# Layer 2's gates by tokens, an earlier x tile, a last gate item between two pooling items, and a margin for TensorE's choice of line

## Chip, core and metric

The kernel runs on one core of one Trainium2 chip. The metric is the device time of one execution in microseconds. The kernel before has a median of 1224.74 us in 3 runs (1224.27 to 1226.64). Its profiled execution took 1224.48 us; the profiled span is 1222.7 us, so 1.78 us lie around the span.

## The reference

Two layers work on 1040 tokens (16 meta tokens and 1024 of the sequence) of width 1024. Each has 4 heads of forgetting attention ("fox"), 4 heads of differential attention and a pooling mixer; they are gated, joined and projected back.

```python
for l in range(DEPTH):                                   # 2 layers
    hn = rmsnorm(h, norm_g[l])
    proj = einsum('bld,de->ble', hn, w_in[l])
    fq, fk, fv, fz, fg, dq, dk, dv, dz, pu, pz = split(proj)
    log_f = log_sigmoid(fg + b_f[l])                     # 4 gates per token
    c = transpose(cumsum(log_f, axis=1))                 # added to the fox scores
    a_out = forgetting_attention(fq, fk, fv, c) * silu(fz)
    b_out = rmsnorm(differential_attention(dq, dk, dv, lam), subln_g[l]) * (1 - lambda_init) * silu(dz)
    c_out = pooling_mixer(pu, w_pool[l], pool_scale[l]) * silu(pz)
    h = h + einsum('ble,ed->bld', concatenate([a_out, b_out, c_out]), w_out[l])
y = rmsnorm(h[:, N_META:N_META + S], final_g)
```

The pooling mixer takes means over windows of 2, 4, 8 and 16 tokens, subtracts the input, multiplies by a 64x64 matrix per group and scales each channel with `pool_scale`.

## The kernel before

**Tiles.** Activations are kept transposed in `HT`, with 1024 channels in 8 blocks of 128 partitions and 1040 tokens along the free axis. Values are split into a high and a low part, and each product is made of three (high by high, high by low, low by high). ACT copies the high part out of PSUM, DVE subtracts it from PSUM to give the low part; for weights ACT makes the high part and POOL the low one (`ws<-wr,ws`). Projections run over the tokens in three chunks of 346 to 348 columns, in blocks of 128 output channels. PSUM tiles are named by use: `psP` projections, `psS` scores and transposes into `HT`, `psT` transposes of probabilities (`p`) and of gates, `psO` attention outputs.

**Stages of a layer.** First come the norm and the transposes into `HT` (in layer 2 these run beside the output projection of layer 1, tile by tile), and the four gates per token. Then six attention units follow, two of fox and four of differential attention; while a unit's attention runs, the projections of the next unit are the filler. Beside unit 5 the filler is a list of items: the z gate of the unit, two pooling items (`pool_item` 1 and 0, each of two groups) and two z gates of the pooling. Last is the output projection.

**The gates.** Layer 1 projects them (`psP<-HT,wg`, 36 columns of weights, three chunks of tokens). Layer 2 sums products on DVE into `gt`, 128 tokens by 9 tiles by 4 gates (`next_gates`, line 743). Its `end()` transposes the nine 128x4 pieces on PE, ACT adds the bias on the way to the row tile `gx` of 4x1040, and `gate_sums` (line 773) makes `mn`, `na`, two passes of ACT (Exp and Ln), a subtraction and a scan along the 1040 tokens. The result `mn` is stored to `c_d` in DRAM by SP and read back as `cb`, spread over 128 partitions, which the fox softmax of DVE adds to the scores (`p<-psS,cb`).

**Meta keys.** `meta_t` (line 1000) transposes the probabilities of the 16 meta tokens into `psT` and makes the tile `ptm` of 96 partitions, which is a high part, a low part and the high part again (lines 1009 to 1011).

**What sets the order.** The program is first written out by a planner. Class `Order` (line 160) then collects every instruction with an estimated duration and plays a list schedule. `prepare` computes from each instruction the longest way to the end. `simulate` takes on each engine the instruction that can start first, the one with the longest way where several can. On PE there are up to six lines, each in its own order, and the choice is only which line goes next. `tell` then fixes this order on the chip. All engines and SP's DMA queue so run in a fixed order, and an instruction that waits holds back what stands behind it on its engine. Matmuls are at line 517 of the profile, transposes on PE at line 523, everything else at line 151.

Of the kernel before, what the change touches and what calls it, by code (L numbers as in the profile page):

```python
# [161 lines left out]
class Order:  # L162
# [5 lines left out]

    def __init__(self):
        self.ops, self.writes, self.reads, self.rings, self.place = [], {}, {}, {}, {}  # L170
        self.stream = 0
# [32 lines left out]
    def add(self, eng, ins, outs, inps, dur, port=False):  # L204
        k, before, names = len(self.ops), set(), set()
        for aps, own, others in ((inps, self.reads, (self.writes,)), (outs, self.writes, (self.writes, self.reads))):
            for ap in aps:
                name = ap.tensor.name
                names.add(name)
                p0, p1, at = self.parts(ap)  # L210
                if self.place.get(name, ("",))[0] == "VM":
                    p0, p1, at = 0, 128, [(0, 1 << 20)]
                for lo, hi in at:
                    for other in others:
                        old = other.get(name, ())
                        before.update(e[4] for e in old if e[2] < hi and lo < e[3] and e[0] < p1 and p0 < e[1])
                        if own is self.writes and old:
                            other[name] = [e for e in old if e[0] < p0 or e[1] > p1 or e[2] < lo or e[3] > hi]
                    own.setdefault(name, []).append((p0, p1, lo, hi, k))
# [16 lines left out]
    def cost(eng, op, out, ins, extra, kw):  # L236
# [16 lines left out]
        if not sbuf or op == "tensor_tensor_scan":  # L253
            return 150 + 1.05 * n, False
# [6 lines left out]
    def prepare(self):  # L261
# [12 lines left out]
        for o in ops:  # L274
            for b in o["before"]:
                ops[b]["after"].append(o["k"])

        last = None
        for o in reversed(ops):
            way = max((ops[a]["way"] for a in o["after"]), default=0.0)  # L280
            for n in o["tiles"]:
                tag, i = self.place[n]
                bufs, names = self.rings[tag]
                if i + bufs < len(names) and self.first[names[i + bufs]] > o["k"]:
                    way = max(way, ops[self.first[names[i + bufs]]]["way"])
            way += o["end"]
            if o["eng"] == "pe":
                if last is not None:
                    way = max(way, last + o["dur"])
                last = way  # L290
            o["way"] = way

    def simulate(self):
        ops = self.ops
        self.prepare()
# [45 lines left out]
        while n_done < len(ops):  # L341
            best = None
            for e in engines:
                if e == "pe":
                    c = None
                    for line in lines.values():
# [3 lines left out]
                        d = (t, 0.0, line[-1], t, e)  # L350
                        if c is None or d < c:
                            c = d
                    if c is None:
                        continue
                else:
# [71 lines left out]
def hymba(  # L427
# [315 lines left out]
    def next_gates(l):  # L743

        bf = small.tile([4, 1], F32, tag="bf", name=nm("bf"), bufs=2)
        sync.dma_start(bf, b_f[l].rearrange("(f o) -> f o", o=1))
        gx = row("gx")[:4]
# [4 lines left out]
        gt = small.tile([128, 9, 4], F32, tag="gt", name=nm("gt"), bufs=1)  # L752
        done = []
# [9 lines left out]
        def end():  # L763
            with ordr.line(4):
                for g, np_, col in done:
                    pt = psT()[:4, :np_]
                    transpose(pt, g, identf[:np_, :np_])
                    act.activation(gx[:, col : col + np_], pt, AF.Identity, bias=bf)
            gate_sums(l, gx)
# [161 lines left out]
    def task_steps(st, jp, m, idx):  # L931
# [70 lines left out]
        def meta_t():  # L1002
# [6 lines left out]
            act.activation(ptm[0:32], pt, AF.Copy)  # L1009
            dve.tensor_tensor(out=ptm[32:64], in0=pt, in1=f32(ptm[0:32]), op=ALU.subtract)  # L1010
            act.activation(ptm[64:96], pt, AF.Copy)
# [454 lines left out]
    HT = big.tile([128, 2, 8, T], F32R, name="HT")  # L1466
    g = load_g(norm_g[0])
# [26 lines left out]
    for l in range(DEPTH):  # L1494
# [29 lines left out]
        for u in range(6):  # L1524
# [6 lines left out]
            else:  # L1531
                Y = []
                more += [pool_item(l, t, Y) for t in (1, 0)] + [pool_gate(l, t, Y) for t in (1, 0)]
# [15 lines left out]
    ordr.simulate()  # L1549
# [42 lines left out]
```

## Time and profile before

| | us |
|---|---|
| median of 3 runs | 1224.74 |
| profiled execution | 1224.48 |
| its span | 1222.7 |
| PE busy | 1188.7 |
| DVE busy | 814.0 |
| ACT busy | 658.3 |
| POOL busy | 493.5 |

An engine is busy while the profile shows an instruction on it. A line of the timeline gives the start, the time until the end of the group, the engine, the source line, the operation, what is written and read, the shape, the count, and in brackets the idle time before it with the instruction that ended it. The waits view sums these idle times. The windows view cuts the span into stretches and gives each engine's busy time in them.

### The profile page before, as it was taken

Reading aid. Unit: us, or ns where it says so; the run is one execution under the profiler, and the core shown is the slowest. Engines: PE = TensorE matmul, PEld = TensorE weight load, DVE = VectorE, ACT = ScalarE, POOL = GpSimd, SP = SyncE. Lnnn points to the kernel's source line nnn. Section 1 sums busy time; section 2 is a strip of 40 time slices with the busy share of each in tenths; the row PEclk is TensorE's granted clock in tenths of the full one; section 3 lists DMA queues with packets and bytes.
Section 4 is the critical chain, followed back from the end, with each engine's and each line's share of the span. In section 5 each row is a group of like instructions: output and inputs, shape, how many; then the busy total and the mean of one; then the engine's idle time right before and its main releaser. Section 6 shows DMA issues by size and latency. Waiting matters only on the chain.

```text
span 1222.7 us, 21035 instructions
## 1 busy us (share of the span) xinstructions
PE 1188.7 (97%) x7605; PEld 1120.7 (92%) x7605; DVE 814.0 (67%) x2137; ACT 658.3 (54%) x1536; POOL 493.5 (40%) x572
## 2 busy tenths in 40 slices
PE   5999999999999999899999999999999999999997
PEld 4999999999999999878889899999999999998886
DVE  6557567675766767667886675676768585777422
ACT  6556556565555654552235565665655555556322
POOL 4331623336162542465425234252443526235532
PEclk9999999999999999999999999999999999999999
DMA  7120211121222263472110212111223223325431
GB/s 244 27 71 18 59 47 27 45 44 32 53 40 61 35 126 78 136 237 80 67 53 18 71 36 69 27 27 53 30 42 61 40 50 65 78 50 158 140 108 52
DMA packets 101273, 84.21 MB, mean 69 GB/s; under 512 B 18296, under 2 KB 90232, under 8 KB 101168
## 3 DMA queue, kind: packets, MB, share of 16 engines
q1 hardware_dynamic: 101024, 82.60, 26.5%
q8 instruction: 60, 0.98, 0.3%
q14 instruction: 45, 0.37, 0.1%
q10 hardware_dynamic: 144, 0.26, 0.1%
HBM read 69.00 MB, written 13.80 MB: 68 GB/s over the span
## 4 chain that ended last, share of the span: by engine, by line
PE 86%; DVE 5%; ACT 3%; DMA 2%; issue 2%; SPq 1%; POOL 1%; POOLq 0%; ACTq 0%; DVEq 0%
PE psP L517 55%; PE psS L517 15%; PE psO L517 8%; PE psT L523 7%; DVE p L151 1%; SPq L151 1%; DMA r_d<-rs 1%; PE psS L523 1%; PE psT L517 1%; ACT K L151 1%; DVE K L151 1%; DMA sc<-in_pool_scale_dram 1%; ACT ptm L151 0%; DMA x<-in_x_dram 0%; DVE ptm L151 0%
## 5 line engine op out<-in xcount | busy, mean ns | idle before, releaser
L517 PE MATMUL psP<-HT,ws 128*128 128x346 f32 (+5 forms) x4032 | 730.3, 325 | 3.9 <-DVE K L151 2.0
L517 PEld LDWEIGHTS psP<-HT,ws 128*128 128x128 f32 x4032 | 636.5, 188 | 6.5 <-issue 2.3
L151 POOL TENSOR_TENSOR ws<-wr,ws 128x512 fp32r<-128x512 f32 x112 | 150.0, 1342 | 263.3 <-ACT ws L151 203.0
L151 POOL TENSOR_TENSOR q<-rq,q 64x256 fp32r<-64x256 f32 (+1 forms) x192 | 147.9, 770 | 124.7 <-DVE q L151 104.2
L151 ACT ACTIVATE p<-p,mx 128x144 f32<-128x144 f32 (+3 forms) x192 | 150.5, 784 | 49.3 <-DVE mx L151 48.3
L517 PE MATMUL psS<-K,q 128*128 128x392 f32 (+9 forms) x696 | 146.7, 324 | 1.0 <-DVE mx L151 0.8
L151 DVE TENSOR_TENSOR pp<-psT,pp 128x512 fp32r<-128x512 f32 (+1 forms) x160 | 99.2, 634 | 46.7 <-ACT pp L151 45.0
L517 PE MATMUL psO<-pp,VV 128*128 128x256 f32 (+1 forms) x800 | 129.2, 283 | 0.2
L523 PE MATMUL psT<-identf,p 128*128 128x128 f32 (+1 forms) x704 | 114.5, 273 | 3.3 <-DVE p L151 3.0
L151 ACT ACTIVATE pp<-psT 128x512 fp32r<-128x512 f32 (+1 forms) x160 | 85.4, 551 | 60.0 <-PE psT L523 55.9
L517 PE MATMUL psP<-HT,ms 128*128 128x512 f32 (+1 forms) x504 | 115.0, 385 | 0.5 <-POOL ms L151 0.3
L517 PEld LDWEIGHTS psO<-pp,VV 128*128 128x128 f32 x800 | 113.1, 189 | 2.0 <-DVE pp L151 0.9
L517 PEld LDWEIGHTS psS<-K,q 128*128 128x128 f32 (+1 forms) x696 | 108.4, 186 | 4.7 <-DVE mx L151 2.7
L517 PEld LDWEIGHTS psP<-HT,ms 128*128 128x128 f32 x504 | 90.7, 188 | 20.7 <-POOL ms L151 0.8
L523 PEld LDWEIGHTS psT<-identf,p 128*128 128x128 f32 (+1 forms) x704 | 81.3, 132 | 10.8 <-DVE p L151 4.7
L151 ACT ACTIVATE ws<-wr 128x512 fp32r<-128x512 f32 x112 | 70.0, 628 | 33.4 <-PE psP L517 18.4
L151 ACT ACTIVATE ptm<-psT 32x256 fp32r<-32x256 f32 (+1 forms) x128 | 47.5, 371 | 63.1 <-DVE ptm L151 45.0
L517 PE MATMUL psS<-HT,ms 128*128 128x512 f32 (+2 forms) x320 | 75.4, 394 | 0.0
L151 DVE TENSOR_SCALAR p<-p,rd 128x144 f32<-128x144 f32 (+7 forms) x128 | 72.3, 568 | 1.7
L517 PEld LDWEIGHTS psS<-HT,ms 128*128 128x128 f32 (+2 forms) x320 | 57.5, 180 | 16.7
L151 DVE TENSOR_TENSOR K<-psP,K 64x346 fp32r<-64x346 f32 (+1 forms) x72 | 37.2, 517 | 47.4 <-ACT K L151 46.8
L151 POOL TENSOR_TENSOR ms<-mr,ms 128x128 fp32r<-128x128 f32 (+2 forms) x39 | 39.1, 1010 | 68.7 <-ACT ms L151 68.6
(138 smaller groups left out, 1423.0 us busy)
## 6 DMA issues: line engine op xcount, KB each, us to landing
wr<-in_w_in_dram SPq DMA_DIRECT2D x112, 256.0 KB, 2.8
wo<-in_w_out_dram SPq DMA_DIRECT2D x14, 512.0 KB, 5.3
mr<-mix_d SPq DMA_DIRECT2D x14, 320.0 KB, 4.5
cb<-c_d SPq DMA_DIRECT2D x8, 520.0 KB
x<-in_x_dram SPq DMA_DIRECT2D x8, 512.0 KB, 6.5
res<-in_x_dram SPq DMA_DIRECT2D x8, 512.0 KB
h_d<-res SPq DMA_DIRECT2D x8, 512.0 KB, 2.6
res<-h_d SPq DMA_DIRECT2D x8, 512.0 KB, 4.6
```

The lines of the kernel that those rows point to most:

```text
L151: r = f(*args, **kw)
L517: r = nc.tensor.matmul(o, w, m, start=start, stop=stop)
L523: r = nc.tensor.transpose(o, src, ident)
```

## The change

1. PE's choice between its lines compares the times at which their heads are ready plus 400 ns (`SPARE`); an instruction that has been ready for less than 400 ns when PE gets free counts as later. The planned start is still the real one.
2. `ptm` counts as one tile in the order's dependencies, and in `meta_t` the second ACT copy stands before DVE's subtraction.
3. The scan has a cost of its own in the order's estimates.
4. `prepare` is split. `weigh` computes the ways, from the second round on in the order of the starts just planned; `choose` runs up to 6 rounds of `weigh` and `simulate` and keeps the round that ends first by the estimates.
5. In layer 2 the bias, the minimum, Exp, Ln and the subtraction of the gates work on `gt` (128x36) before the nine transposes. Behind the transposes only ACT's copies, the scan and the store remain.
6. The x tile 0 is loaded ahead of `g`.
7. Beside unit 5 the items are pool item 1, z gate of the unit, pool item 0, and the two pooling gates; before, the z gate came first.

```diff
+    SPARE = 400
...
-                if self.place.get(name, ("",))[0] == "VM":
+                if self.place.get(name, ("",))[0] in ("VM", "ptm"):
...
-        if not sbuf or op == "tensor_tensor_scan":
+        if op == "tensor_tensor_scan":
+            return 150 + 2.1 * n, True
+        if not sbuf:
             return 150 + 1.05 * n, False
...
+    def weigh(self):
+        ops, last = self.ops, None
+        for o in reversed(ops if self.start is None else sorted(ops, key=lambda o: (self.start[o["k"]], o["k"]))):
+            after = o["after"] + [self.first[self.heir[n]] for n in o["tiles"] if n in self.heir]
+            way = max((ops[a].get("way", 0.0) for a in after), default=0.0) + o["end"]
             if o["eng"] == "pe":
                 if last is not None:
                     way = max(way, last + o["dur"])
                 last = way
             o["way"] = way
+    def choose(self, rounds):
+        self.prepare()
+        best = None
+        for _ in range(rounds):
+            self.weigh()
+            end = self.simulate()
+            if best is None or end < best[0]:
+                best = end, self.start, self.done, self.taken, self.order
+            self.heir = {old: n for n, old in self.taken.items() if old}
+        _, self.start, self.done, self.taken, self.order = best
...
                         t = max(free["pe"], ready[line[-1]] + 20, s + 20)
-                        d = (t, 0.0, line[-1], t, e)
+                        sure = max(free["pe"], ready[line[-1]] + self.SPARE, s + self.SPARE)
+                        d = (sure, 0.0, line[-1], t, e)
...
+                    c = (c[3], *c[1:])
...
         def end():
+            gx = row("gx")[:4]
+            flat = gt.rearrange("p n f -> p (n f)")
+            mn = sm("mn", 36)
+            dve.tensor_tensor(out=gt, in0=gt, in1=bf.unsqueeze(1).to_broadcast([128, 9, 4]), op=ALU.add)
+            dve.tensor_scalar(out=mn, in0=flat, scalar1=0.0, scalar2=None, op0=ALU.min)
+            dve.scalar_tensor_tensor(out=flat, in0=mn, scalar=2.0, in1=flat, op0=ALU.mult, op1=ALU.subtract)
+            act.activation(flat, flat, AF.Exp)
+            act.activation(flat, flat, AF.Ln, bias=1.0)
+            dve.tensor_tensor(out=flat, in0=flat, in1=mn, op=ALU.subtract)
             with ordr.line(4):
                 for g, np_, col in done:
                     pt = psT()[:4, :np_]
                     transpose(pt, g, identf[:np_, :np_])
-                    act.activation(gx[:, col : col + np_], pt, AF.Identity, bias=bf)
-            gate_sums(l, gx)
+                    act.activation(gx[:, col : col + np_], pt, AF.Copy)
+            mn = row("mn")[:4]
+            dve.tensor_tensor_scan(
+                out=mn, data0=one[:4].to_broadcast([4, T]), data1=gx, initial=0.0, op0=ALU.mult, op1=ALU.add)
+            sync.dma_start(c_d[l], mn)
...
             act.activation(ptm[0:32], pt, AF.Copy)
+            act.activation(ptm[64:96], pt, AF.Copy)
             dve.tensor_tensor(out=ptm[32:64], in0=pt, in1=f32(ptm[0:32]), op=ALU.subtract)
-            act.activation(ptm[64:96], pt, AF.Copy)
...
+    load_x(2)
     g = load_g(norm_g[0])
     load_x(5)
...
-                more += [pool_item(l, t, Y) for t in (1, 0)] + [pool_gate(l, t, Y) for t in (1, 0)]
+                more = [pool_item(l, 1, Y), *more, pool_item(l, 0, Y)] + [pool_gate(l, t, Y) for t in (1, 0)]
...
-    ordr.simulate()
+    ordr.choose(6)
     ordr.tell(tc)
```

**Start of the program, PE.** `x_104` and `x_157` are the fourth and fifth x tile on their way into `HT`, `psP_296` is the first of the three gate chunks, `psP_330` the first values of fox. PE in order, before:

```order
L523 MATMUL psS_289<-identf,x_104 128x128 x4
L523 MATMUL psS_316<-identf,x_157 128x128 x2
L517 MATMUL psP_296<-HT,wg_138 36x348 x16
L523 MATMUL psS_316<-identf,x_157 128x128 x2
L523 MATMUL psS_323<-identf,x_157 128x128 x4
L517 MATMUL psP_330<-HT,ws_149 128x400 x12
L517 MATMUL psP_330<-HT,ws_154 128x400 x12
```

And PE at the same place now:

```order
L540 MATMUL psS_289<-identf,x_104 128x128 x4
L534 MATMUL psP_296<-HT,wg_138 36x348 x16
L534 MATMUL psP_330<-HT,ws_149 128x400 x12
L534 MATMUL psP_330<-HT,ws_154 128x400
L540 MATMUL psS_316<-identf,x_157 128x128 x4
L540 MATMUL psS_323<-identf,x_157 128x128 x4
L534 MATMUL psP_330<-HT,ws_154 128x400 x11
```

The gate chunk and 13 value matmuls now stand ahead of the transposes of `x_157`.

**Layer boundary, SP.** `c_d<-mn` stores the running sums of layer 2's gates, `cb` reads them back, `wr` are weight loads, `h_d<-res` stores a tile of layer 1's output. SP in order, before:

```order
L151 DMA wr_8146<-in_w_in_dram 128x4x128
L151 DMA wr_8308<-in_w_in_dram 128x4x128
L151 DMA wr_8313<-in_w_in_dram 128x4x128
L151 DMA c_d<-mn_7967 4x1040
L151 DMA cb_8164<-c_d 128x1040
L151 DMA cb_8166<-c_d 128x1040
```

And SP at the same place now:

```order
L151 DMA wr_8147<-in_w_in_dram 128x4x128
L151 DMA c_d<-mn_7975 4x1040
L151 DMA cb_8165<-c_d 128x1040
L151 DMA cb_8167<-c_d 128x1040
L151 DMA wr_8309<-in_w_in_dram 128x4x128
L151 DMA wr_8314<-in_w_in_dram 128x4x128
```

The store and the two reads now stand ahead of two weight loads that stood ahead of them.

**Pooling of layer 1, ACT.** `th` is a z gate's tanh, `sq` a square of attention outputs, `Y<-psP_6568,sc_6493` takes the pooled product out of PSUM with the channel scale `sc`. ACT in order, before:

```order
L151 ACTIVATE ws_6383<-wr_6381 128x512
L151 ACTIVATE th_6582<-psP_6540 128x346
L151 ACTIVATE sq_6587<-psO_6448 128x256
L151 ACTIVATE Y_5965<-psP_6568,sc_6493 128x348
L151 ACTIVATE Y_5965<-psP_6616,sc_6493 128x346
```

And ACT at the same place now:

```order
L151 ACTIVATE p_6529,den_6543<-p_6529,mx_6530 128x1040
L151 ACTIVATE Y_5715<-psP_6568,sc_6493 128x348
L151 ACTIVATE th_6582<-psP_6512 128x346
L151 ACTIVATE sq_6587<-psO_6453 128x256
L151 ACTIVATE Y_5715<-psP_6616,sc_6493 128x346
```

The first pooled product is now taken out of PSUM ahead of the tanh and the square, not behind them. The scale's DMA `sc` of the first pooling item also moves on SP, from behind the transfers `r_d` and `vr` of the preceding unit to ahead of them.

## Rows read from the trace of the kernel before

**Rows 1.** The page, part 1: engine, busy us (share of span), instructions.

```profile
PE 1188.7 (97%) x7605; PEld 1120.7 (92%) x7605; DVE 814.0 (67%) x2137; ACT 658.3 (54%) x1536; POOL 493.5 (40%) x572
```

**Rows 2.** Windows: stretch and its length, busy time of each engine, PE clock, DMA.

```profile
20.00:45.00 25.00, 22.73 (x139) 20.55 (x140) 15.99 (x30) 13.05 (x29) 11.77 (x14) 0.93 0.28 77
...
480.00:500.00 20.00, 18.41 (x119) 17.71 (x118) 15.16 (x38) 11.56 (x23) 7.69 (x7) 1.00 0.26 64
...
500.00:540.00 40.00, 38.03 (x231) 34.75 (x230) 27.21 (x54) 26.01 (x67) 21.77 (x27) 1.00 0.63 204
...
672.00:690.00 18.00, 15.72 (x105) 15.04 (x103) 8.83 (x23) 9.53 (x21) 5.60 (x4) 1.00 0.34 105
...
1080.00:1110.00 30.00, 27.71 (x182) 26.80 (x181) 25.27 (x60) 17.29 (x35) 13.06 (x12) 1.00 0.34 93
...
1204.00:1222.70 18.70, 12.03 (x75) 10.35 (x73) 6.12 (x10) 3.62 (x9) 2.81 (x6) 0.94 0.15 57
```

**Rows 3.** PE's waits: what for, us in total, times, longest us.

```profile
PE psS L523 <- DMA identf<-in_ident_dram: 10.1, 1, 10.1
```

**Rows 4.** Timeline, start of the program: start us, us, engine, operation [idle before].

```profile
5.76 1.27 DVE L151 SCALAR_TENSOR_TENSOR x<-x,rs,g 16x1024 f32<-16x1024 f32 x1 [3.72 <-DMA g<-in_norm_g_dram]
...
7.09 1.06 ACT L151 ACTIVATE junk<-x 128x1024 bf16<-128x1024 f32 x1 [3.15 <-DMA x<-in_x_dram]
...
18.80 1.07 DVE L151 CAST wg<-wrg 128x32 fp32r<-128x32 f32 x1
...
19.78 2.35 DVE L151 SCALAR_TENSOR_TENSOR x<-x,rs,g 128x1024 f32<-128x1024 f32 x1
...
22.27 0.51 PE L523 MATMUL psS<-identf,x 128*128 128x128 f32 x2 [2.83 <-DVE wg L151]
...
22.44 4.33 PE L517 MATMUL psP<-HT,wg 128*36 128x348 f32 x16
```

**Rows 5.** Timeline, PE: second of three gate chunks in layer 1.

```profile
37.13 2.74 PE L517 MATMUL psP<-HT,wg 128*36 128x346 f32 x16
```

**Rows 6.** Timeline, layer boundary, several engines.

```profile
663.87 0.36 ACT L151 ACTIVATE gx<-psT,bf 4x128 f32<-4x128 f32 x1
...
666.67 0.83 DVE L151 TENSOR_SCALAR mn<-gx 4x1040 f32<-4x1040 f32 x1
...
675.64 2.31 DVE L151 TENSOR_TENSOR_SCAN mn<-gx,na 4x1040 f32<-4x1040 f32 x1
...
678.65 7.53 PE L517 MATMUL psP<-HT,ws 128*128 128x346 f32 x46 [2.03 <-DVE K L151]
...
679.47 0.40 SPq L151 DMA_DIRECT2D c_d<-mn  x1
...
681.91 0.83 SPq L151 DMA_DIRECT2D cb<-c_d  x2
...
686.06 0.31 DVE L151 CUSTOM_DVE_ANT_0 p<-psS,cb 128x144 f32<-128x144 f32 x1 [2.32 <-DMA cb<-c_d]
```

**Rows 7.** Timeline, pooling at the end of either layer: PE, DVE and POOL.

```profile
474.93 1.24 DVE L151 TENSOR_TENSOR wa<-Y 128x1039 f32<-128x1039 f32 x1 [0.39 <-ACT Y L151]
...
492.89 1.29 POOL L151 TENSOR_TENSOR ws<-wr,ws 128x512 fp32r<-128x512 f32 x1
...
492.92 2.35 DVE L151 TENSOR_TENSOR wa<-Y 128x1039 f32<-128x1039 f32 x1
...
496.93 0.15 DVE L151 TENSOR_SCALAR sc<-sc 128x1 f32<-128x1 f32 x1 [1.66 <-DMA sc<-in_pool_scale_dram]
...
497.73 0.75 PE L517 MATMUL psP<-pu,wps 128*128 128x346 f32 x3 [1.21 <-ACT Y L151]
...
511.18 1.86 PE L517 MATMUL psP<-HT,ws 128*128 128x348 f32 x10 [1.53 <-DVE th L151]
...
1104.35 4.14 DVE L151 SCALAR_TENSOR_TENSOR p<-p,n,p 128x912 f32<-128x912 f32 x2
...
1108.55 0.55 PE L523 MATMUL psT<-identf,p 128*128 128x128 f32 x3 [1.83 <-DVE p L151]
```

**Rows 8.** The tile ptm: who waited for it, us, times.

```profile
  PEld psO L517: 4.2, 13
```

More of the change, by code (lines that the diff above doesn't have):

```diff
@@ L276, in prepare @@
                 ops[b]["after"].append(o["k"])
[L278 to L286, printed above, removed]
+        self.start, self.heir = None, {}
+        for bufs, names in self.rings.values():
+            self.heir.update(zip(names, names[bufs:]))
+    def weigh(self):
[3 more added lines that the diff above has]
+            way = max((ops[a].get("way", 0.0) for a in after), default=0.0) + o["end"]
             if o["eng"] == "pe":
@@ L291, in prepare @@
             o["way"] = way
+    def choose(self, rounds):
[8 more added lines that the diff above has]
+        _, self.start, self.done, self.taken, self.order = best
     def simulate(self):
         ops = self.ops
-        self.prepare()
         left = [len(o["before"]) for o in ops]
@@ L743, in next_gates @@
     def next_gates(l):
-        bf = small.tile([4, 1], F32, tag="bf", name=nm("bf"), bufs=2)
-        sync.dma_start(bf, b_f[l].rearrange("(f o) -> f o", o=1))
-        gx = row("gx")[:4]
+        bf = small.tile([128, 4], F32, tag="bfr", name=nm("bf"), bufs=1)
+        sync.dma_start(bf, b_f[l].partition_broadcast(128))
         gw = [sb.tile([128, D], F32, tag="q", name=nm("gw"), bufs=4) for _ in range(4)]
@@ L752, in next_gates @@
         gt = small.tile([128, 9, 4], F32, tag="gt", name=nm("gt"), bufs=1)
+        dve.memset(gt, 0.0)
         done = []
```

## The prediction

> **What bounds the kernel.** The first view is the busy time by engine. PE is busy 1188.7 of 1222.7 us, 97% [rows 1], so the other engines count only where they make PE wait. PE idles 1222.7 - 1188.7 = 34.0 us. The waits of PE give 10.1 of these to the time before its first matmul, which needs the identity matrix from DRAM [rows 3]. The windows give the last stretch 18.70 - 12.03 = 6.67 us [rows 2], in which final tiles are normed and stored. Some 34.0 - 10.1 - 6.7 = 17.2 us are left between. No matmul is removed, so about 17.2 us is all that another order can win. The reader should see in the windows that this idle time stands in few places: pooling of layer 1 (20.00 - 18.41 = 1.59 and 40.00 - 38.03 = 1.97), boundary of the layers (18.00 - 15.72 = 2.28), pooling of layer 2 (30.00 - 27.71 = 2.29) [rows 2], and the start, with one wait of 2.83 [rows 4]. The timeline then tells which instruction is late in each.
>
> **Start.** PE waits 2.83 us at 22.27 for the transposes of the fifth x tile, and the gate chunk stands behind them at 22.44 [rows 4]. What they wait for on DVE is the multiply at 19.78, here 2.35 us long, which ends at 22.13; the low part of wg follows it. In the new order the gate chunk needs no fifth tile. DVE makes wg first, so by the row of the CAST wg could be ready at 18.80 + 1.07 plus a short subtraction, some 20.1. Against it, the multiply of the fourth tile moves behind two evacuations into HT, which makes its transposes, ahead of the gate chunk, later by about one multiply, 1.27 (the size of the one at 5.76 [rows 4]). If this lateness adds in full, the gate chunk starts at about 20.1 + 1.27 = 21.4. I take 22.44 - 21.4 = 1.1 us, -1.1. The bounds are 22.44 - 20.1 = -2.3 and, if the later transposes cost more than the wait gives, +0.5.
>
> The gate chunk itself takes 4.33 us there [rows 4] and 2.74 for one of nearly the same size later [rows 5]; the granted clock of the window from 20 to 45 us is 0.93 [rows 2], so part of it ran at the lower of the two levels, after PE had idled. I leave these 4.33 - 2.74 = 1.6 us in the sum, since a wait of some size remains ahead of the chunk.
>
> Loading x tile 0 ahead of g I cost at nothing. The first DVE multiply waits for g until 5.76, and ACT waits for x until 7.09 [rows 4]. With their places changed g comes about 7.09 - 5.76 = 1.3 later, the multiply of the meta tile (1.27) ends near 5.76 + 1.3 + 1.3 = 8.4, and PE cannot begin before the identity matrix at 10.1 [rows 3], which keeps its place in the queue. That cover is 1.7 us; beyond it every delay of g is a delay of PE.
>
> **Layer boundary.** The chain to be seen: the last copy into gx ends at 663.87 + 0.36 = 664.23, the first operation of the sums starts at 666.67, the scan at 675.64, the reads of cb are issued at 681.91; the first fox softmax of layer 2 starts at 686.06 after 2.32 of waiting for them [rows 6]. The scan holds DVE 2.31 us, and behind it stands the evacuation of K for which PE waits 2.03 until 678.65. In the new order the passes between 666.67 and 675.64, 8.97 us with their waits, are done ahead of the transposes on 36 columns instead of 1040. The scan then follows the last copy. From the scan's start to the softmax takes 686.06 - 675.64 = 10.42, so without delay cb is there at 664.23 + 10.42 = 674.65, 11.4 us sooner. No row has these operations at 36 columns: they cost between 0 and the 8.97 of the wide ones, and as the columns are 36 of 1040 I take it near the lower end. Even at 8.97 cb comes 2.4 sooner, about the 2.32 that DVE waits now. SP keeps this, as the store and the reads pass the two weight loads.
>
> What is late next: ACT stands with a row of the fox softmax that waits for cb ahead of a z gate's tanh, so a late cb would now hold a PSUM bank too. And the scan still stands between two evacuations of K on DVE, only some 11 us earlier, where PE is in a long run of projections. Of the stretch's 2.28 I take -2.0; bounds -2.3 and +2.3 (the scan's whole 2.31 turned into a PE wait at the new place).
>
> **Pooling.** In layer 1 PE waits 1.21 at 497.73 for ACT's Y, which waits for the channel scale that DVE can treat only at 496.93, when its DMA has landed [rows 7]. That DMA stands on SP behind the preceding unit's norm factors; now it stands ahead of them for the first pooling item. At 511.18 PE waits 1.53 for a gate product, with Y behind the tanh on ACT; now Y is ahead. Both belong to the 1.59 + 1.97 of these windows. In layer 2 PE waits 1.83 at 1108.55 [rows 7] for the second of two DVE products p that together took 4.14; now other PE work stands before these transposes. The whole is 1.59 + 1.97 + 2.29 = 5.85. Between the two pooling items PE now has the z gate's projections, while DVE makes the windows of the second. I take three quarters, -4.4; bounds -5.85 and +2.7, the latter if nothing is won and the z gate, one item later, holds up the unit's first outputs by as much as the two waits of layer 1 cost now (1.21 + 1.53 = 2.74).
>
> **Margin, ptm, rounds.** With the ACT copy before DVE's subtraction ptm is complete about one DVE operation sooner. The weight loads of the meta products waited 4.2 us in 13 cases [rows 8], PE itself less, so -1.0; bounds -4.2 and 0. The margin makes PE prefer work that has been ready for some time, and the rounds choose another order throughout. In the idle time outside the places above, 17.2 - 2.8 - 2.3 - 5.85 = 6.3, it can win or lose; I take -0.5 for it, and +1.0 for waits that a new order brings. Bounds for both together -3 and +3.
>
> **Sum.** -1.1 - 2.0 - 4.4 - 1.0 - 0.5 + 1.0 = -8.0. Against the profiled execution of 1224.48 (1222.7 and 1.78 around the span) this gives 1216.5. The median of the runs is 0.26 above the profiled execution, which I neglect.
>
> **Rivals.** *Half comes back.* The gains are there, but a new order brings new waits on the single bank of attention outputs or on DVE: 1224.5 - 4 = 1220.5. For it speaks that the idle time of PE is already small and each wait removed shows the next. Against it, the waits named have single causes that the new rows remove.
>
> *No change.* The stalls of PE move on, because DVE, with 25.27 of 30.00 busy in layer 2's pooling [rows 2], is what lies under them there: 1224. For it speaks that p at 1104.35 was late by DVE itself, and none of its work is removed there.
>
> *Slower.* The window sums of pooling run on DVE with two inputs from SBUF. One took 1.24 at 474.93 and 2.35 at 492.92, beside a POOL instruction at 492.89 of 1.29 [rows 7], 1.11 more. If the new order puts the four sums of the pooling item that now comes first beside POOL in both layers, DVE is 8 x 1.11 = 8.9 late. Lost to PE in full in place of the pooling gain, with the other terms kept at -3.6, it gives 1224.5 - 3.6 + 8.9 = 1229.8; it decides from the point where more than 3.6 of the 8.9 reaches PE. For it speaks the pair of rows, against it that PE has projections as filler.
>
> The Trainium skill has a rule on this (SBUF — State Buffer, Who interferes with whom): a DVE instruction with two SBUF inputs and a POOL instruction that reads SBUF lock each other out, whichever starts first. The rows agree: the sum grew by 1.11, somewhat less than the 1.29 of the POOL instruction. By the rule's full lock, at 1.29 each, the eight sums would be 10.3 late and the time 1231.2.
>
> *More than forecast.* PE's clock stays up at the start (-1.6), and pooling, boundary and ptm give most of their bounds: 1224.5 - 1.1 - 1.6 - 2.3 - 5.5 - 3.0 - 1.0 = 1210.
>
> **Chances.** Forecast 0.54 (1216.5, its own range 1212 to 1219), half 0.18, no change 0.11, slower 0.08, more 0.09. A measurement of this kernel tells a difference from no change at about 0.2%, 2.4 us, that is 1222.3 to 1227.1. Forecast and more are faster whole, 0.63, and of the half 0.15: 0.78. The same: 0.03 of the half, 0.09 of no change, 0.01 of slower: 0.13. Slower: 0.07 of the slower and 0.02 of no change: 0.09. For 8 in 10 the range leaves out the slower case above 1224.5 and what lies under 1209; the unknown costs reach to 1207 below by the idle time.
>
> **What would show it.** In the changed profile the wait of 2.83 at the start should be about 1.1 shorter and the gate chunk start near 21.4; cb should land before 678 and DVE wait for it under 1 us; PE's waits for ACT's Y and for the tanh product in layer 1's pooling should be gone; ACT should no longer wait for DVE's part of ptm; PE's idle time should be near 26. The prediction is wrong if PE's busy time itself changes by more than 2 us, if the sums of the windows take over 2 us each, or if the idle time stands again in the same windows.

## The result, and the profile after

| | before | after |
|---|---|---|
| median, us | 1225.24 (1224.27 to 1226.64, 4 runs) | 1206.97 (1205.17 to 1208.09, 4 runs) |
| ratio to before | 1 | 0.9849 [0.9832, 0.9866] |
| profiled span | 1222.7 | 1205.4 |
| PE busy | 1188.7 | 1179.2 |
| PE idle | 34.0 | 26.2 |

The kernel became 18.3 us faster; 8.0 were forecast, and the time lies below the range, whose lower end was 1209. The forecast also named what would show it wrong: a change of PE's busy time by more than 2 us. The page of the changed kernel, part 1, answers to [rows 1]:

```profile
PE 1179.2 (98%) x7605; PEld 1120.6 (93%) x7605; DVE 806.7 (67%) x2138; ACT 658.7 (55%) x1536; POOL 491.3 (41%) x572
```

The number of matmuls is the same, 7605, and PE is busy 9.5 us less, where the forecast allowed 2. So more than half of the 17.3 us that the span lost was not idle time in the profile of before. The windows of the changed kernel answer to [rows 2] (the program is ahead of before by some 6 us at the first pooling and 17 at the second, so equal windows do not hold quite the same work):

```profile
20.00:45.00 25.00, 24.87 (x156) 23.08 (x157) 15.49 (x31) 14.43 (x31) 12.69 (x16) 1.00 0.28 76
...
480.00:500.00 20.00, 20.00 (x135) 19.76 (x134) 18.15 (x45) 10.43 (x20) 5.34 (x5) 1.00 0.27 72
500.00:540.00 40.00, 38.31 (x221) 32.79 (x221) 23.18 (x46) 25.53 (x65) 21.96 (x30) 1.00 0.72 227
...
672.00:690.00 18.00, 18.00 (x121) 17.90 (x120) 11.70 (x41) 10.50 (x27) 4.01 (x4) 1.00 0.16 40
...
1080.00:1110.00 30.00, 30.00 (x208) 29.61 (x207) 23.97 (x46) 21.33 (x45) 11.62 (x15) 1.00 0.46 137
...
1187.00:1205.40 18.40, 11.82 (x74) 10.26 (x72) 5.91 (x10) 3.62 (x9) 2.81 (x6) 0.88 0.15 58
```

Boundary and second pooling have no idle PE left, the first pooling 1.69 in place of 3.56, and the tail is as it was (6.58, was 6.67). At the start the granted clock is 1.00 from 20 to 45 us, where it was 0.93.

**Where busy time hid.** A matmul's record runs past the point where the next one could begin, so a late start shows as idle only in part. In the changed kernel a matmul of 346 columns is recorded with 324 ns on average, while from its start to the next start it is 159 ns in the median. A place of before shows it, once by PE and once by the weight loads (start, length of the group, and in brackets the idle time before it):

```profile
850.97 0.60 PE L523 MATMUL psT<-identf,p 128*128 128x128 f32 x4
851.79 0.36 PE L517 MATMUL psT<-s,onesr 128*128 128x256 f32 x1 [0.22 <-DVE s L151]
```

```profile
850.80 0.54 PEld L523 LDWEIGHTS psT<-identf,p 128*128 128x128 f32 x4
851.76 0.19 PEld L517 LDWEIGHTS psT<-s,onesr 128*128 128x128 f32 x1 [0.43 <-PE psT L523]
```

The four transposes start at 850.97 and the next matmul 0.82 later. At the pace of undisturbed stretches four transposes take about 0.44, so 0.38 were lost; PE shows 0.22 of it and the weight loads 0.43. By this pair, a start that is late by less than about 0.38 - 0.22 = 0.16 us does not show as idle time of PE at all.

I therefore take a lost time from the starts alone: for each matmul the time to the next start, less the larger of 109 ns and columns / 2.4 ns + 15 ns, a yardstick fitted to undisturbed stretches of these traces. It gives 109, 159 and 228 ns for 128, 346 and 512 columns; the medians of the changed kernel are 108, 159 and 232. The yardstick is 1170.6 us for every kernel here; small negative sums mean a pace slightly better than it. In the first attention stage 36 matmuls of 16 columns follow one another faster than it, which makes that column too small by 2.3 us, in before and after alike. Cut at equal amounts of matmul work (50, 450, 600, 700 and 1050 us of it), the lost time in us is:

| profiled run | start | attention 1 | pooling 1 and out | boundary | attention 2 | pooling 2 and out | sum |
|---|---|---|---|---|---|---|---|
| before | 9.2 | 5.3 | 7.8 | 4.6 | 3.7 | 5.0 | 35.5 |
| after | 8.0 | 4.0 | 4.5 | 0.1 | 0.4 | 1.5 | 18.5 |
| difference | -1.1 | -1.3 | -3.4 | -4.4 | -3.3 | -3.5 | -17.0 |

From PE's first start to its last end before was 1206.1 us; 17.4 of it were idle, and 35.5 - 17.4 = 18.1 more were lost inside busy time. After it is 9.9 and 8.6. About 1.6 of the 18.1 (4.33 - 2.74, [rows 4] and [rows 5]) is the gate chunk at the lower clock; by this yardstick the rest is late starts. So the forecast's ceiling of 17.2 was half of what was lost.

**The start.** The timeline of the changed kernel, PE and DVE, answers to [rows 4]:

```profile
18.71 1.27 DVE L151 SCALAR_TENSOR_TENSOR x<-x,rs,g 128x1024 f32<-128x1024 f32 x1
...
19.91 0.17 DVE L151 CAST wg<-wrg 128x32 fp32r<-128x32 f32 x1
...
20.11 0.19 DVE L151 TENSOR_TENSOR wg<-wrg,wg 128x32 fp32r<-128x32 f32 x1
...
20.13 1.94 PE L540 MATMUL psS<-identf,x 128*128 128x128 f32 x8 [2.69 <-DVE wg L151]
...
21.73 3.51 PE L534 MATMUL psP<-HT,wg 128*36 128x348 f32 x16
```

The wait of 2.83 is not shorter but stands one tile earlier (2.69, for the fourth tile; the profile names wg, but the tile's multiply, which ends at 19.98, is what these transposes read), as DVE now evacuates two blocks of HT first. The gate chunk starts at 21.73 (before 22.44, forecast 21.4) and takes 3.51 instead of 4.33.

**The boundary**, answering to [rows 6]:

```profile
659.47 0.27 ACT L151 ACTIVATE gx<-psT 4x128 f32<-4x128 f32 x1
...
660.88 2.30 DVE L151 TENSOR_TENSOR_SCAN mn<-one,gx 4x1040 f32<-4x1040 f32 x1
...
663.21 0.27 SPq L151 DMA_DIRECT2D c_d<-mn  x1
...
664.95 0.82 SPq L151 DMA_DIRECT2D cb<-c_d  x2
...
670.05 0.31 DVE L151 CUSTOM_DVE_ANT_0 p<-psS,cb 128x144 f32<-128x144 f32 x1 [2.10 <-DMA cb<-c_d]
```

From the last copy to the scan it is now 1.1 us and was 11.4. DVE still waits 2.10 for cb, but nothing on PE waits behind it.

### The profile page after: what moved, and what is told of

Same layout as the page of the kernel before. It is cut to its first block, busy times and chain, and to the rows that moved or that the text cites. A ratio compares the mean times of both kernels' runs of the same rounds, so it can differ in the third digit from the quotient of the medians.

```text
span 1205.4 us, 21078 instructions
## 1 busy us (share of the span) xinstructions
PE 1179.2 (98%) x7605; PEld 1120.6 (93%) x7605; DVE 806.7 (67%) x2138; ACT 658.7 (55%) x1536; POOL 491.3 (41%) x572
## 4 chain that ended last, share of the span: by engine, by line
PE 92%; DMA 3%; DVE 2%; ACT 1%; SPq 1%; issue 1%; POOL 0%; POOLq 0%; DVEq 0%; ACTq 0%
PE psP L534 60%; PE psS L534 15%; PE psO L534 8%; PE psT L540 8%; PE psS L540 1%; SPq L151 1%; DMA vr<-r_d 1%; PE psT L534 1%; DMA wo<-in_w_out_dram 1%; DMA x<-in_x_dram 1%; DVE p L151 1%; DMA wp<-in_w_pool_dram 0%; DMA rs<-v 0%; DMA r_d<-rs 0%; DVE K L151 0%
## 5 line engine op out<-in xcount | busy, mean ns | idle before, releaser
L151 POOL TENSOR_TENSOR ws<-wr,ws 128x512 fp32r<-128x512 f32 x112 | 154.6, 1382 | 253.9 <-ACT ws L151 164.7
L151 POOL TENSOR_TENSOR q<-rq,q 64x256 fp32r<-64x256 f32 (+1 forms) x192 | 145.0, 755 | 114.5 <-DVE q L151 92.3
L534 PE MATMUL psS<-K,q 128*128 128x392 f32 (+9 forms) x696 | 150.4, 324 | 2.3 <-DVE mx L151 2.2
L151 DVE CUSTOM_DVE_ANT_0 p<-psS,dist 128x272 f32<-128x272 f32 (+7 forms) x128 | 61.0, 490 | 10.3 <-PE psS L534 6.7
L151 ACT ACTIVATE ms<-mr 128x128 fp32r<-128x128 f32 (+2 forms) x40 | 16.4, 416 | 86.5 <-PE psS L534 33.0
```

What stands on the lines that cost most here:

```text
L151: r = f(*args, **kw)
L534: r = nc.tensor.matmul(o, w, m, start=start, stop=stop)
```

## The experiments

Three theories on the 10 us that the forecast missed: M, the margin removes short waits all over, which the profile counts as busy; N, only the named stalls count; R, the rounds of replanning carry it. In the second set theory P says that the time is the plan's end, as the planner estimates it, plus a gap. All kernels ran in turn with the kernel before, and ratios are to it. Its median was 1225.2, 1225.0, 1226.5 and 1225.3 us in the four sets, so kernels of different sets are better compared by their ratios; a difference of 1.5 us between their medians can be one between the sets.

| kernel | plan's end, us | median us | ratio [95%] | start | att. 1 | pool 1 | bound. | att. 2 | pool 2 |
|---|---|---|---|---|---|---|---|---|---|
| before | 1203.6 | 1225.2 | 1 | 9.2 | 5.3 | 7.8 | 4.6 | 3.7 | 5.0 |
| after | 1198.9 | 1207.0 | 0.9849 [0.9832, 0.9866] | 8.0 | 4.0 | 4.5 | 0.1 | 0.4 | 1.5 |
| a_spare | 1209.1 | 1220.8 | 0.9959 [0.9946, 0.9973] | 8.7 | 2.9 | 4.0 | 4.6 | -0.8 | 12.9 |
| a_plan | 1203.4 | 1207.7 | 0.9855 [0.9842, 0.9868] | 10.8 | 1.0 | 4.4 | 1.4 | -0.8 | 2.0 |
| a_prog | 1200.0 | 1220.2 | 0.9959 [0.9945, 0.9973] | 8.2 | 8.5 | 4.4 | 1.9 | 2.8 | 3.3 |
| u_rounds | 1201.6 | 1215.2 | 0.9918 [0.9905, 0.9931] | 8.4 | 2.9 | 9.4 | 0.6 | 0.9 | 3.2 |
| u_gates | 1198.9 | 1208.6 | 0.9856 [0.9841, 0.9871] | 8.2 | 3.6 | 3.7 | 3.0 | 0.6 | 1.5 |
| u_items | 1206.2 | 1214.0 | 0.9897 [0.9881, 0.9914] | 8.4 | 2.5 | 3.5 | 0.3 | -0.9 | 11.3 |
| u_load | 1201.7 | 1213.3 | 0.9891 [0.9876, 0.9905] | 11.0 | 4.9 | 4.6 | 0.0 | 0.9 | 1.5 |
| u_ptm | 1198.8 | 1209.8 | 0.9865 [0.9845, 0.9885] | 8.2 | 1.2 | 4.8 | 0.5 | 0.7 | 3.8 |
| rounds2 | 1199.3 | 1209.3 | 0.9863 [0.9846, 0.9879] | 8.2 | 4.6 | 5.1 | 0.0 | 0.6 | 1.6 |
| round5 | 1200.4 | 1208.4 | 0.9856 [0.9841, 0.9872] | 8.5 | 2.8 | 8.0 | 0.0 | 0.8 | 1.5 |
| spare600 | 1198.7 | 1204.1 | 0.9816 [0.9801, 0.9831] | 8.3 | 3.1 | 2.8 | -0.3 | -1.8 | 3.6 |
| noheir | 1198.3 | 1211.7 | 0.9874 [0.9855, 0.9893] | 8.3 | 3.4 | 7.2 | 1.1 | 0.6 | 2.3 |

The six right-hand columns are the lost time of the profiled run in us.

**The planner and the program apart.**

a_spare, the kernel before with the margin, and with ptm counted as one tile:

```diff
+    SPARE = 400
...
-                if self.place.get(name, ("",))[0] == "VM":
+                if self.place.get(name, ("",))[0] in ("VM", "ptm"):
...
-                        d = (t, 0.0, line[-1], t, e)
+                        sure = max(free["pe"], ready[line[-1]] + self.SPARE, s + self.SPARE)
+                        d = (sure, 0.0, line[-1], t, e)
...
+                    c = (c[3], *c[1:])
```

> The kernel before with the margin of 400 ns in PE's choice of line alone (and ptm counted as one tile). Theory M, the part of the gain that the prediction missed (about 9 us) comes from short waits all over the attention stages, which the margin removes and which the profile counts as busy PE: PE busy falls by 5 to 9 us from 1188.7, time 1215 to 1220. Theory N, only the named stalls at the start, the layer boundary and the pooling count, and the margin is worth little: PE busy within 1.5 us of 1188.7, time 1222 to 1226.

It took 1220.8, and PE was busy 1184.5, 4.2 less, so neither theory holds in full: theory M wanted 5 to 9 us less and at most 1220, theory N at most 1.5 less and at least 1222. The two attention stages lost 2.2 in place of 9.0, which is theory M's effect with 6.8 us. The second pooling gave most of it back (12.9 in place of 5.0), in one place, by the timeline of this kernel on DVE, ACT and PE:

```profile
1090.10 1.17 DVE L151 SCALAR_TENSOR_TENSOR p<-p,n,p 128x912 f32<-128x912 f32 x1
...
1091.30 0.41 DVE L151 TENSOR_TENSOR ptm<-psT,ptm 32x256 fp32r<-32x256 f32 x1
...
1092.14 0.37 ACT L151 ACTIVATE ptm<-psT 32x256 fp32r<-32x256 f32 x1
...
1092.57 0.58 PE L521 MATMUL psO<-ptm,VM 96*128 96x256 f32 x1 [6.30 <-ACT ptm L151]
...
1094.43 3.83 PE L521 MATMUL psP<-HT,ws 128*128 128x346 f32 x12 [1.07 <-ACT Y L151]
```

DVE's subtraction for ptm stands behind other work, ACT's second copy behind it, and PE behind that. Whether the margin or the counting of ptm as one tile put it there was not tried apart. The next 12 matmuls take 3.83 where 12 of this size took 2.17 at a like place of before:

```profile
1097.29 2.17 PE L517 MATMUL psP<-HT,ws 128*128 128x346 f32 x12 [0.29 <-ACT Y L151]
```

The clock fell: the granted clock of 1080 to 1110 us is 0.83 in this kernel, by its windows, and was 1.00 [rows 2].

```profile
1080.00:1110.00 30.00, 22.63 (x133) 22.00 (x132) 16.05 (x36) 12.87 (x26) 9.46 (x10) 0.83 0.42 120
```

a_plan, the kernel before with the whole new planner: `SPARE`, the scan's cost, ptm as one tile, `weigh` and `choose(6)`, and none of the other edits (all its planner edits are in the diff of the change).

```diff
...
-    ordr.simulate()
+    ordr.choose(6)
```

> The kernel before with the whole new planner (margin, scan cost, ptm as one tile, six rounds), but the old gates, old load order, old items and old order of the ptm copies. Theory M: 1212 to 1217, the steady stages like those of the changed kernel, boundary and pooling as before. Theory N: 1221 to 1226. Theory R, the rounds of replanning carry it, also at boundary and pooling: 1208 to 1212.

It took 1207.7, as fast as the changed kernel. This is theory R and beyond it: the planner alone, with the old gates, items, loads and copies, gives the whole gain; its interval covers nearly the same stretch as that of the changed kernel. The planner here is margin, rounds, the scan's cost and ptm as one tile together; the last two were not tried by themselves. The boundary lost 1.4 there in place of 4.6, with the old chain of the sums, so another order hides most of it.

a_prog, the changed kernel with the old way of choosing:

```diff
-    SPARE = 400
+    SPARE = 20
...
-    ordr.choose(6)
+    ordr.choose(1)
```

> The changed kernel with the margin at 20 ns and one round, that is with the old way of choosing, and the new gates, load order, items, ptm copies and scan cost. Theory M: 1213 to 1218, boundary and pooling gains kept, short waits of the attention stages back. Theory N: 1207 to 1210. Theory R: 1216 to 1222.

It took 1220.2, in the range of theory R. Under the old way of choosing the new program, with the scan's cost and ptm as one tile, gives 4.8 us (1225.0 to 1220.2); under the new one it gives no difference that these runs can tell (a_plan 1207.7, after 1207.0). By place the program does there much as was forecast of it: the start loses 1.0 less, the boundary 2.7 and the poolings 5.1 (forecast 1.1, 2.0 and 4.4). But the attention stages lose 11.3, which is 2.3 more than before. Its plan ends at 1200.0, 1.1 later than that of the changed kernel, and the chip comes 20 us after it.

u_rounds, the changed kernel with one round:

```diff
-    ordr.choose(6)
+    ordr.choose(1)
```

> The changed kernel with one round of planning instead of six, margin and all else kept. Theory M and N: 1206 to 1209, the rounds are worth under 2 us. Theory R: 1211 to 1218.

It took 1215.2, so the rounds are worth 8.2 us, as theory R says. The margin is the difference to a_prog, 5.0 us. With it the attention stages lose 7.5 less (11.3 to 3.8), and the first pooling 5.0 more (4.4 to 9.4). What the rounds add is in the poolings: with one round PE waits in the first for the pooled values pu and for a product p, and the granted clock falls, by the timeline of PE and the windows:

```profile
504.70 0.43 PE L534 MATMUL psP<-pu,wps 128*128 128x348 f32 x1 [1.44 <-ACT pu L151]
...
507.93 1.76 PE L540 MATMUL psT<-identf,p 128*128 128x128 f32 x7 [2.81 <-DVE p L151]
```

```profile
500.00:520.00 20.00, 15.75 (x93) 15.24 (x92) 9.22 (x22) 9.45 (x20) 8.10 (x9) 0.83 0.49 167
```

In the changed kernel the only larger wait of this stage is this one:

```profile
529.21 0.39 PE L534 MATMUL psT<-s,onesr 128*128 128x256 f32 x1 [1.33 <-POOL s L151]
```

What the margin removes shows when each kernel's plan is set beside its trace. In the two attention stages PE has 5151 matmuls. The plan of before lets 240 of them start less than 0.4 us after the moment at which, by its estimates, the last thing they wait for is ready. The time lost ahead of these 240 is 9.4 us, which is all that these stages lost (9.0; the others are slightly better than the yardstick). In a_prog it is 251 matmuls and 11.3 of 11.3 us. With the margin only 5 such matmuls are left in a_spare and 3 in u_rounds, with 0.5 and 0.1 us. Over the whole of before, 340 of the 7605 matmuls have so little slack, and 28.4 of the 35.5 us stand ahead of them. So the short waits stood where the plan had no slack, and the margin takes such starts out of the plan.

**One edit undone at a time**, under the new planner.

u_gates has the old `next_gates`, with bias and sums behind the transposes:

```diff
-            dve.tensor_tensor(out=gt, in0=gt, in1=bf.unsqueeze(1).to_broadcast([128, 9, 4]), op=ALU.add)
...
-                    act.activation(gx[:, col : col + np_], pt, AF.Copy)
+                    act.activation(gx[:, col : col + np_], pt, AF.Identity, bias=bf)
+            gate_sums(l, gx)
...
```

> The changed kernel with the old gates of layer 2 (passes over 4x1040 behind the transposes). Theory P, the planner hides what it knows and the time is the plan's end plus a gap: its plan ends at 1198.9, as that of the changed kernel, so 1205 to 1209 and no PE wait at the layer boundary. Theory N, the long chain itself makes PE wait at the boundary, as it did before: 1209 to 1212, with a wait for K or mx of 2 us or more there.

It took 1208.6, and its interval overlaps that of the changed kernel almost whole. The place is nevertheless clear: the boundary lost 3.0 in place of 0.1, and PE waits there for K and for mx, the maxima of the scores, by its timeline:

```profile
670.67 9.87 PE L534 MATMUL psP<-HT,ws 128*128 128x346 f32 x59 [1.19 <-DVE K L151]
...
681.67 0.52 PE L534 MATMUL psS<-K,q 128*128 128x272 f32 x2 [1.14 <-DVE mx L151]
```

So the time is in theory P's range and just under theory N's, while theory P's claim of no wait at the boundary fails. Theory N has the place right, with 2.9 us; its waits are two of 1.1 to 1.2 and not one of 2. In the whole the scatter between orders covers most of it.

u_items has the z gate first again:

```diff
-                more = [pool_item(l, 1, Y), *more, pool_item(l, 0, Y)] + [pool_gate(l, t, Y) for t in (1, 0)]
+                more += [pool_item(l, t, Y) for t in (1, 0)] + [pool_gate(l, t, Y) for t in (1, 0)]
```

> The changed kernel with the old order of items beside unit 5 (the z gate first). Theory P: its plan ends at 1206.2, 7.3 later than that of the changed kernel, so 1211 to 1217, the loss in both poolings. Theory N, as in the prediction (4.4 for both poolings): 1210 to 1213. Theory R, the rounds make up for it, as they did in the kernel with the new planner alone (1207.7 with the same items): 1206 to 1209.

It took 1214.0, above the ranges of theories N and R. Theory P's 1211 to 1217 holds in time, but not in place: the loss is in the second pooling alone (11.3 in place of 1.5; the first has 3.5 in place of 4.5). PE waits there four times for 5.9 us together, and from 1082.8 to 1093.1 it runs at the lower clock, from the third of these waits on:

```profile
1080.60 0.39 PE L534 MATMUL psO<-ptm,VM 96*128 96x256 f32 x1 [0.66 <-DVE ptm L151]
...
1082.36 0.36 PE L534 MATMUL psT<-s,onesr 128*128 128x256 f32 x1 [1.26 <-DVE s L151]
...
1084.04 0.58 PE L534 MATMUL psT<-s,onesr 128*128 128x256 f32 x1 [1.33 <-POOL s L151]
...
1087.25 3.83 PE L534 MATMUL psP<-HT,ws 128*128 128x346 f32 x12 [2.63 <-ACT Y L151]
```

```profile
1080.00:1110.00 30.00, 24.19 (x137) 23.45 (x138) 16.43 (x37) 16.17 (x37) 15.47 (x19) 0.83 0.33 104
```

a_plan has the same old items and loses 2.0 there. The order of items by itself is therefore not what costs it; the order that the planner makes of it here is.

u_load has g ahead of x tile 0 again:

```diff
-    load_x(2)
     g = load_g(norm_g[0])
```

> The changed kernel with g loaded ahead of x tile 0 again. Theory P: its plan ends at 1201.7, 2.7 later, so 1208 to 1212, the loss before 50 us. Theory N, as in the prediction (load order worth nothing): 1206 to 1208.

It took 1213.3, above theory P's range by a little. At the start 3.0 us more are lost than in the changed kernel: the gate chunk starts at 24.88 for 21.73, and the granted clock of the window is 0.84 in place of 1.00, by timeline and windows of this kernel:

```profile
24.88 1.35 PE L534 MATMUL psP<-HT,wg 128*36 128x348 f32 x4 [1.60 <-DVE wg L151]
```

```profile
20.00:45.00 25.00, 22.33 (x130) 19.46 (x131) 14.83 (x30) 12.36 (x26) 11.74 (x14) 0.84 0.28 80
```

a_plan, with the same old load order, has the same start (10.8), and the nine kernels with the margin and the new load order have 8.0 to 8.5. The load that the forecast cost at nothing is worth some 3 us under this planner. PE's first matmul is not later for it (9.83, in the changed kernel 9.90). The order changes instead: ahead of the gate chunk PE has 48 transposes of x in u_load and a_plan and 40 in the changed kernel, so with g first the planner again puts the fifth tile's transposes ahead of the chunk, where two of them stood in before. In profiled spans the difference to the changed kernel is 4.3; the rest is spread.

u_ptm has the second copy behind the subtraction:

```diff
-            act.activation(ptm[64:96], pt, AF.Copy)
             dve.tensor_tensor(out=ptm[32:64], in0=pt, in1=f32(ptm[0:32]), op=ALU.subtract)
+            act.activation(ptm[64:96], pt, AF.Copy)
```

> The changed kernel with the second ACT copy of ptm behind DVE's subtraction again (ptm still one tile in the order). Theory P: its plan ends at 1198.8, so 1205 to 1209. Theory N, as in the prediction (1.0, at most 4.2): 1207 to 1211, with more waiting of the weight loads for ptm.

It took 1209.8 (1207.8 to 1212.1, a wide scatter), and its profiled span is 1206.0 against 1205.4. It lies in theory N's range and just above theory P's, and its interval overlaps that of the changed kernel. The weight loads wait 1.5 us for ptm in the changed kernel, 2.4 here, and 4.2 in before [rows 8]; the changed kernel first:

```profile
  PEld psO L534: 1.5, 2
```

```profile
  PEld psO L534: 2.4, 3
```

So of the 2.7 us by which this wait fell, the copy's place gives 0.9 and the planner the rest. Whether it gives 0 or 2 us of the whole stays open.

**The rounds and the margin.**

rounds2 and round5 change how many rounds there are and which is kept:

```diff
-    ordr.choose(6)
+    ordr.choose(2)
```

> The changed kernel with two rounds of planning instead of six; its plan ends at 1199.3 (six rounds 1198.9, one round 1201.6). If one weighing by the planned starts does the work, 1205 to 1209, with the poolings as short as in the changed kernel. If the best of many rounds is what counts, 1211 to 1215, as with one round.

```diff
-            if best is None or end < best[0]:
+            if True:
...
-    ordr.choose(6)
+    ordr.choose(5)
```

> The changed kernel with the fifth round's order, which the rule would not keep: its plan ends at 1200.4, the latest of the five reweighed ones. If the time follows the plan plus the gap of 8 of the changed kernel, 1208 to 1209. If each order falls by chance and the plan's end tells little within 2 us, anywhere from 1205 to 1214; the place of the loss then differs from round to round.

They took 1209.3 and 1208.4. rounds2 is just above its first range (1205 to 1209) and clear of the second, with the poolings nearly as short as in the changed kernel (5.1 and 1.6). One weighing by the planned starts gives 5.9 of the 8.2 us of the rounds; whether the other four give anything is not shown, as the intervals overlap. That the best of six is kept matters little, as the fifth, which the rule would not keep, is as fast. Within 2 us the plan's end says little: round5's lies 1.1 later than that of rounds2, and it is not slower. Its loss stands elsewhere, 8.0 in the first pooling.

noheir does not update, from round to round, which tile follows which in a buffer:

```diff
-            self.heir = {old: n for n, old in self.taken.items() if old}
```

> The changed kernel without the update of which tile follows which in a buffer between rounds; its plan ends at 1198.3, the earliest of all. If the plan's end decides, 1205 to 1207. If the slots are what the weighing needs, 1209 to 1214, with waits for buffers (psP, psO) in the pooling.

It took 1211.7 with the earliest plan of all (1198.3), so the plan's end does not decide, and 2.7 more are lost in the first pooling than in the changed kernel. The time is in its second range, but the waits for buffers expected with it did not show: apart from the start, PE's largest wait is 2.8 us for sums of squares (psT from DVE s), in two pieces. The intervals of noheir and rounds2 overlap, so its cost against one reweighing is not shown.

spare600 raises the margin:

```diff
-    SPARE = 400
+    SPARE = 600
```

> The changed kernel with a margin of 600 ns; its plan ends at 1198.7. Theory M, a margin keeps the chip near the plan: PE's lost time in the attention stages at or under the 4.4 us of the changed kernel, the whole 1203 to 1207. If 400 was enough, 1206 to 1208. If a larger margin costs order elsewhere, 1209 to 1213, the loss at the pooling.

It took 1204.1, ratio 0.9816 [0.9801, 0.9831], faster than the changed kernel (0.9849 [0.9832, 0.9866]) by intervals that just don't meet. Theory M's range holds, and not the one for 400 being enough. The attention stages lost 1.3 in place of 4.4, and PE was busy 1177.0:

```profile
PE 1177.0 (98%) x7605; PEld 1120.5 (93%) x7605; DVE 813.6 (68%) x2138; ACT 658.3 (55%) x1536; POOL 496.3 (41%) x572
```

This is the fastest kernel of the study. The changed kernel with six rounds and a margin of 20 was not run, so what the margin is worth under six rounds stays open.

## Why the prediction was wrong

**The ceiling.** "About 17.2 us is all that another order can win" is the step that failed first. PE's busy time was taken as work. It held 18.1 us of lost time, late starts but for about 1.6, and more than half of the gain came from there (9.5 of 17.3). PE's idle time came out at 26.2 where the forecast had 26, but that is luck: a_plan, without the edits whose gains the forecast added up, has 1205.7 - 1180.1 = 25.6.

**The margin and the rounds.** "I take -0.5 for it, and +1.0 for waits that a new order brings" is the term that was mis-sized most. Margin and rounds together are worth 13.2 us on the new program (a_prog to after); on the old one they are worth 17.3, there with the scan's cost and ptm as one tile (before to a_plan). The forecast read the change as edits to single places and the planner as noise. It is the other way round. A plan that takes PE's next instruction at the moment at which it is estimated ready is late on the chip wherever the estimate is short: in before 240 such starts carry all that the attention stages lost. Why the rounds help is shown by place alone, the poolings (9.4 and 3.2 lost with one round, 4.5 and 1.5 with six); what in the weighing does it stays open. The gap between plan and chip is 21.6 in before and 20.2 in a_prog, 11.7 and 13.6 with the margin in one round, and 4.3 and 8.1 with the rounds too.

**Start.** -1.1 forecast, -1.1 measured in lost time, and 0.2 more from an earlier first start (9.90 for 10.10). That the two agree is partly luck. The gate chunk came at 21.73 for 21.4, 0.7 sooner than before, and the wait stayed (2.69) and moved to the fourth tile. The chunk itself took 0.8 less, as the granted clock no longer fell, which only the rival "more" had. The clock is no sure effect of the change: with the same loads a_prog, u_items, u_ptm and round5 have 0.90 to 0.91 in this window, and their start loses 8.2 to 8.5, little more. The load order, costed at nothing with a cover of 1.7 us, is worth 3.0 by u_load. The cover held for PE's first matmul, for which it was worked out; what it left out is that the load decides whether the planner puts the fifth tile ahead of the gate chunk.

**Boundary.** -2.0 forecast, at most -2.3; -4.4 measured. The window of [rows 2] held 2.28 of idle time; 4.6 were lost in the stretch. The mechanism was right, with 2.9 us of it by u_gates, but a_plan's order loses only 1.4 with the old gates. The forecast of cb before 678 held (670.05); that DVE would wait under 1 us for it did not (2.10).

**Pooling.** -4.4 forecast, at most -5.85; -6.9 measured (with the output projections). Both waits in layer 1 named in the forecast are gone, and layer 2's too. That the order of items brings this is not shown: a_plan loses 6.4 with the old items and the changed kernel 6.0.

**ptm.** ACT no longer waits for DVE's part (45.0 us in before), as forecast; DVE now waits 23.2 us for ACT's copies. The weight loads' wait fell by 2.7 us, 0.9 of it by the copy's place; the forecast's -1.0 lies within what u_ptm leaves open.

**The rivals.** The slower one did not come: eight sums late by 1.11 were its price, and of the twelve window sums of both layers, into wa and wb, one was slowed, by 0.74 us. The tile wb in the changed kernel (least, median and longest duration in ns), and the two instructions on DVE and POOL:

```profile
L151 DVE TENSOR_TENSOR wb<-wa x6: 1225/1230/1972, 460.9 to 1082.2; 128x1038 f32<-128x1038 f32 x2, 64x1032 f32<-64x1032 f32 x2, 64x1038 f32<-64x1038 f32 x2
```

```profile
1082.18 1.97 DVE L151 TENSOR_TENSOR wb<-wa 64x1038 f32<-64x1038 f32 x1
```

```profile
1082.15 0.91 POOL L151 TENSOR_TENSOR Y<-Y,th 128x332 f32<-128x332 f32 x1 [2.81 <-DVE th L151]
```

The rule of the Trainium skill (SBUF — State Buffer, Who interferes with whom), that one of two such instructions waits for the other to end, agrees with this pair: DVE starts 0.03 after POOL and takes 0.74 longer, somewhat less than the 0.88 that POOL still ran.

The rival "more" was nearest, at 1210, and had the wrong reasons for most of its terms.

## What to carry to other kernels

Where an engine is 97% busy, measure its lost time from start to start against the pace of an undisturbed run, since idle time shows only the part of a late start that the record before it does not cover. In a fixed order, weigh an edit of the planner by the gap between its plan and the chip, and try a margin for readiness even if it makes the plan longer: here 400 ns, with ptm as one tile, lengthened the plan from 1203.6 to 1209.1 us and shortened the run by 4.2. Judge edits under such a planner by place and not by the total alone, since another order moves the total by several us.

## What was not expected of the hardware

A wait can cost more than its length. In a_spare the granted clock fell within a wait of 6.30 us, in u_items at the start of the third of four waits of 5.9 us together. The next 12 matmuls took 3.83 us in place of 2.17, with a granted clock of 0.83 in the window against 1.00.

How long a wait must be for this, these runs do not settle. At the start the clock stayed at 1.00 in the changed kernel after waits of 0.68 and 2.69 us. In u_items, with the same work and waits of 0.77 and 2.76 us, the window from 20 to 45 us has 0.91:

```profile
19.38 1.94 PE L540 MATMUL psS<-identf,x 128*128 128x128 f32 x8 [2.76 <-DVE wg L151]
```

```profile
20.00:45.00 25.00, 25.00 (x153) 22.71 (x152) 15.21 (x29) 13.61 (x30) 12.05 (x14) 0.91 0.27 75
```

In u_load, where five waits of 0.5 to 1.6 us follow one another (0.54, 1.14, 1.26, 0.58, 1.60), it has 0.84; the clock there fell at 17.7, just after the second of them, so the later ones did not cause the fall.
